# Block 4 of the output: six rows of 16 partitions stored in transfers of three partitions

## The chip, the cores and the metric

The kernel runs on one core of a Trainium2 chip. Its time is the device time of one execution in microseconds (us). Four runs of the kernel before took 162.29 to 163.43 us, with a median of 163.08. A further execution was taken by the hardware profiler: its time was 162.68 us and its span, from the first to the last instruction, 161.4 us.

## What is computed

A linear layer whose weight is built first, from a matrix, a low-rank product and a norm of each column:

```python
def reference(x, W, lora_A, lora_B, m, scale):
    W_adapted = W + scale * (lora_A @ lora_B)
    W_norm = np.sqrt(np.sum(W_adapted ** 2, axis=0, keepdims=True) + 1e-8)
    W_final = W_adapted / W_norm * m
    return (x.reshape(-1, 256) @ W_final).reshape(16, 2048, 256)
```

x has 32,768 rows of 256 float32 numbers, 33.55 MB, and the output is as large. W is 256 x 256, the rank is 16.

## The kernel before

**Blocks and chunks.** The rows are cut into 8 blocks of 4096. A block is 4 MB (4096 KB): 128 partitions with 32 rows each, and the 32 rows of a partition lie one behind the other in memory, 32 KB in one piece. A block has eight chunks of 4 rows per partition, so there are 64 chunks, g = 0 to 63. Five buffers in on-chip memory hold a block each (`x_bufs`); block b uses buffer b mod 5.

**The path of a chunk.** SP (SyncE) issues the loads of x. GpSimd rounds a pair of chunks to bf16 (L208). TensorE transposes it (L321), VectorE copies the transposed pair out of PSUM (L248), and TensorE multiplies it with the finished weight (L335). ScalarE (ACT) copies each product from PSUM back to where the chunk of x was (L276), so that the output of a block takes the place of its input in the buffer. At the last chunk of a store ACT drains (L282) and issues the store (L146). The loads stand in one queue (q1, from SP), the stores in another (q10, from ACT). Both are worked off by the same 16 DMA engines.

**The list of stores.** Each entry of `stores` has its first chunk, the number of chunks, the rows that one transfer takes, and the chunk after which ACT issues it. By number:

- 0 and 1: blocks 0 and 1, due at chunks 19 and 20
- 2 and 3: block 2 in two parts, due at chunk 24
- 4, 5 and 6: block 3, as four transfers of 4 rows, one of 4 rows, and one of 12 rows, due at chunks 27, 28 and 44
- 7: block 4, chunks 32 to 39, all 32 rows in one transfer of 4096 KB, due at chunk 44 together with store 6
- 8 and 9: blocks 5 and 6, due at chunks 47 and 55
- 10 and 11: block 7 in two halves, due at chunks 59 and 63

**Waits.** SP waits for stores 0 to 3 before it loads into their buffers again; GpSimd waits for store 2. Stores 4 to 11 have semaphores of their own (`late`), and nothing in the kernel waits for them but SP at the very end, at L360, one after the other. A transfer adds 16 to the semaphore of its store; `pieces` says what a store's semaphore has reached when all of it has landed.

**Where the change sits.** `transfer` cuts an entry into transfers of `rows` rows over all 128 partitions, and issues them on the engine that it is given.

Of the kernel before, what the change touches and what calls it, by code (L numbers as in the profile page):

```python
# [11 lines left out]
def kernel(  # L12
# [11 lines left out]
    P = 128  # L24
# [91 lines left out]
    stores = [(b * CH, CH, CH * J, 19 + b) for b in range(F - 1)]  # L116
    stores += [(G - CH, 3, 3 * J, G), (G - 5, 5, 5 * J, G)]
    FIRST = len(stores)
    stores += [(G, 4, J, G + 3), (G + 4, 1, J, G + 4)]
    stores += [(G + 5, CH - 5, (CH - 5) * J, 44), (G + CH, CH, CH * J, 44)]  # L120
    stores += [(b * CH, CH, CH * J, (b + 1) * CH - 1) for b in range(F + 2, NBLK - 1)]
# [1 line left out]

    def pieces(entry):

        return 16 * (entry[1] * J // entry[2])


    late = [nc.alloc_semaphore(f"store{n}") for n in range(FIRST, len(stores))]
    sems = {f"store{FIRST + k}": s for k, s in enumerate(late)}  # L130

    def sem(name):
        if name not in sems:
            sems[name] = tc.alloc_semaphore(name)
        return sems[name]

    def transfer(engine, name, entry, dram, store):
        g0, cnt, rows = entry[:3]
        b, c = divmod(g0, CH)
        (u0, ucnt), = [u for u in units if u[0] <= g0 < u[0] + u[1]]  # L140
        unit = dram[u0 * J * P : (u0 + ucnt) * J * P].rearrange("(p j) k -> p j k", p=P)
        for r in range(0, cnt * J, rows):
            here = x_bufs[b % XBUFS][:, c * J + r : c * J + r + rows, :]
            there = unit[:, (g0 - u0) * J + r : (g0 - u0) * J + r + rows, :]
            src, dst = (here, there) if store else (there, here)
            engine.dma_start(out=dst, in_=src).then_inc(sem(name), 16)  # L146

    def load_x(n):
        transfer(nc.sync, f"load{n}", loads[n], x_flat, False)

    def store_y(n):
        transfer(nc.scalar, f"store{n}", stores[n], out_flat, True)

    def wait_load(engine, g):
        engine.wait_ge(sem(f"load{load_of[g]}"), pieces(loads[load_of[g]]))

    def wait_store(engine, n):
        engine.wait_ge(sem(f"store{n}"), pieces(stores[n]))
# [3 lines left out]
        out=w_nat[:], in_=W.rearrange("(p t) o -> p t o", t=KC)  # L162
    ).then_inc(sem("load_w"), 16)
    nc.scalar.dma_start(
        out=a_nat[:], in_=lora_A.rearrange("(p t) r -> p t r", t=KC)
# [3 lines left out]
    for n in range(len(loads)):  # L169
# [14 lines left out]
        out=identity[:],  # L184
        in_=zeros[:],
# [7 lines left out]
    for p in range(1, NPR):  # L193
# [10 lines left out]
        if p == REST:  # L204
            wait_store(nc.gpsimd, FIRST - 2)
        if p >= NXB:
            nc.gpsimd.wait_ge(sem("turned"), p - NXB + 1)
        nc.gpsimd.tensor_copy(  # L208
            out=xb_bufs[p % NXB][:],
            in_=x_bufs[b % XBUFS][:, 2 * c * J : 2 * (c + 1) * J, :],  # L210
# [15 lines left out]
        out=wa[:], in0=ab_ps, scalar=float(scale), in1=w_nat[:], op0=ALU.mult, op1=ALU.add  # L226
# [19 lines left out]
    for p in range(NPR):  # L246
        nc.vector.wait_ge(sem("turned"), p + 1)
        nc.vector.tensor_copy(  # L248
            out=xt_bufs[p % NXT][:].rearrange("p r t -> p (r t)").bitcast(FP32),
            in_=xt_ps[p % 2][:],  # L250
# [4 lines left out]
    for engine, idle in ((nc.gpsimd, 8), (nc.vector, 24)):  # L255
# [13 lines left out]
        out=norm[:], in_=n2_ps, func=AF.Sqrt, bias=eps_col[:]  # L269
    ).then_inc(sem("act"), 1)  # L270
    drains = 0
    for g in range(NCH):
# [4 lines left out]
            out=x_bufs[b % XBUFS][:, c * J : (c + 1) * J, :], in_=y_ps[g % 2][:]  # L277
# [80 lines left out]
    for k, s in enumerate(late):  # L358
        nc.sync.wait_ge(s, pieces(stores[FIRST + k]))
        nc.sync.sem_clear(s)  # L360
# [35 lines left out]
```

## Time and profile before

| what | value |
|---|---|
| median of 4 runs (lowest, highest) | 163.08 us (162.29, 163.43) |
| profiled execution: time, span | 162.68 us, 161.4 us |
| PE (matmul) busy | 96.3 us, 60% of the span |
| ACT busy | 66.1 us, 41% |
| GpSimd busy | 60.8 us, 38% |
| VectorE busy | 45.0 us, 28% |
| HBM read, written | 33.85 MB, 33.55 MB |
| first, last issue of a load of x | 1.4 us, 85.8 us |
| first, last issue of a store | 47.0 us, 131.4 us |

Busy time is the sum of an engine's instructions without the issuing of DMAs. A row of digits on the page has one digit for each fortieth of the span, which here is 4.03 us; each is the busy share in tenths, and 9 is 90% or more. The DMA row is the mean over the core's 16 DMA engines. The compute engines have nothing more to do after 131.8 us; what follows is stores alone. Times inside the profile count from the start of the span.

### The profile page before, as it was taken

The numbers are of one execution on the slowest core, as the hardware profiler recorded it, in microseconds if no ns is written. First come the engines' busy times: TensorE is split into PE (matmuls) and PEld (weight loads), VectorE is DVE, ScalarE is ACT, GpSimd is POOL, SyncE is SP. The second block draws the span as 40 slices with busy tenths as digits, with TensorE's granted clock in tenths as the row PEclk, the third lists the DMA queues.
The fourth block names the chain that finished last, engine by engine and source line by source line (L and its number), as shares of the span: only waits on it lengthen the run. The fifth ranks groups of instructions, "written<-read, shape, count | busy, mean of one in ns | idle before, by whom it ended". The sixth has DMA issues, their size and how long they took to land. (4 is left out here: it accounts for less than half of the span.)

```text
span 161.4 us, 2027 instructions
## 1 busy us (share of the span) xinstructions
PE 96.3 (60%) x786; PEld 85.0 (53%) x786; DVE 45.0 (28%) x44; ACT 66.1 (41%) x68; POOL 60.8 (38%) x38
## 2 busy tenths in 40 slices
PE   0695936999999720000699999989997920000000
PEld 0284925899998610000689999979986910000000
DVE  0567322335353500000115354436353300000000
ACT  3411840686767450000056867766865740000000
POOL 1045319568685000001938685845829100000000
PEclk9999997899999995555559999999999997555555
DMA  4999999999999999989999999999999999999995
GB/s 158 427 455 463 390 504 406 390 495 414 422 390 455 422 422 439 439 370 447 412 418 425 436 418 425 447 419 424 440 484 398 439 457 400 439 455 406 410 430 223
DMA packets 4645, 67.43 MB, mean 418 GB/s; under 512 B 657, under 2 KB 674, under 8 KB 1698
## 3 DMA queue, kind: packets, MB, share of 16 engines
q1 hardware_dynamic: 2304, 33.82, 49.3%
q10 hardware_dynamic: 2338, 33.59, 48.9%
q14 instruction: 3, 0.02, 0.0%
HBM read 33.85 MB, written 33.55 MB: 418 GB/s over the span
## 5 line engine op out<-in xcount | busy, mean ns | idle before, releaser
L276 ACT COPY x_sb<-y_ps 128x1024 f32<-128x1024 f32 x64 | 62.3, 1014 | 58.8 <-PE y_ps L335 57.1
L208 POOL CAST xb<-x_sb 128x2048 bf16<-128x2048 f32 x31 | 58.4, 1893 | 63.9 <-DMA out_dram<-x_sb 24.7
L335 PE MATMUL y_ps<-w_final,xt 128*128 128x256 bf16 x512 | 64.6, 281 | 3.7 <-PEq L311 3.6
L248 DVE COPY xt<-xt_ps 128x1024 f32<-128x1024 f32 x32 | 39.1, 1225 | 75.2 <-PE xt_ps L321 75.0
L335 PEld LDWEIGHTS y_ps<-w_final,xt 128*128 128x128 bf16 x512 | 51.4, 101 | 11.4 <-issue 4.6
L321 PE MATMUL xt_ps<-identity,xb 128*128 128x128 f32 x264 | 37.3, 289 | 24.9 <-PEq L311 24.9
L321 PEld LDWEIGHTS xt_ps<-identity,xb 128*128 128x128 f32 x264 | 32.7, 151 | 26.4 <-issue 25.8
L292 PE MATMUL y_ps<-identity,a_nat 128*16 128x128 f32 x2 | 0.6, 396 | 4.1 <-DMA a_nat<-in_lora_A_dram 4.1
L264 ACT CAST xb<-x_sb 128x2048 bf16<-128x2048 f32 x1 | 1.9, 1898 | 2.5 <-DMA x_sb<-in_x_dram 2.5
L262 ACT ACT_TABLE_LOAD x1 | 1.3, 1283 | 2.4 <-issue 2.4
L292 PEld LDWEIGHTS y_ps<-identity,a_nat 128*16 128x16 f32 x2 | 0.1, 88 | 4.1 <-issue 4.1
L238 DVE RECIPROCAL rnorm<-norm 128x256 f32<-128x256 f32 x1 | 1.8, 1753 | 1.3 <-ACT norm L268 1.3
L305 PE MATMUL y_ps<-sq,ones 128*128 128x256 f32 x4 | 2.1, 674 | 0.0
L214 POOL MEMSET xb<- 128x2048 bf16 x1 | 1.8, 1804 | 0.0
L305 PEld LDWEIGHTS y_ps<-sq,ones 128*128 128x128 f32 x4 | 1.2, 324 | 0.8 <-DVE sq L229 0.7
L301 PE MATMUL y_ps<-m_row,ones 1*128 1x256 f32 x2 | 1.2, 709 | 0.5 <-DMA m_row<-in_m_dram 0.5
L220 DVE CAST b_bf<-b_nat 16x256 bf16<-16x256 f32 x1 | 0.3, 281 | 3.5 <-DMA b_nat<-in_lora_B_dram 3.5
L268 ACT ACTIVATE norm<-y_ps,eps_col 128x256 f32<-128x256 f32 x1 | 0.5, 474 | 1.6 <-PE y_ps L305 1.6
L296 PE MATMUL y_ps<-b_bf,aT 16*128 16x256 bf16 x2 | 0.6, 404 | 0.8 <-DVE aT L222 0.8
L301 PEld LDWEIGHTS y_ps<-m_row,ones 1*128 1x128 f32 x2 | 0.5, 305 | 1.0 <-DMA m_row<-in_m_dram 1.0
L225 DVE SCALAR_TENSOR_TENSOR wa<-y_ps,w_nat 128x512 f32<-128x512 f32 x1 | 0.7, 691 | 0.8 <-PE y_ps L296 0.8
L296 PEld LDWEIGHTS y_ps<-b_bf,aT 16*128 16x128 bf16 x2 | 0.1, 107 | 1.2 <-DVE aT L222 1.2
(14 smaller groups left out, 4.4 us busy)
## 6 DMA issues: line engine op xcount, KB each, us to landing
out_dram<-x_sb ACTq DMA_DIRECT2D x5, 4096.0 KB, 26.8
x_sb<-in_x_dram SPq DMA_DIRECT2D x7, 2048.0 KB, 29.7
x_sb<-in_x_dram SPq DMA_DIRECT2D x3, 4096.0 KB, 29.9
out_dram<-x_sb ACTq DMA_DIRECT2D x2, 2048.0 KB, 30.1
x_sb<-in_x_dram SPq DMA_DIRECT2D x1, 3072.0 KB, 46.5
out_dram<-x_sb ACTq DMA_DIRECT2D x2, 1536.0 KB, 19.3
out_dram<-x_sb ACTq DMA_DIRECT2D x1, 2560.0 KB, 30.8
out_dram<-x_sb ACTq DMA_DIRECT2D x5, 512.0 KB, 38.1
```

Of the source, the lines that this page charges most:

```text
L208: nc.gpsimd.tensor_copy(out=xb_bufs[p % NXB][:], in_=x_bufs[b % XBUFS][:, 2 * c * J : 2 * (c + 1) * J, :],).then_inc(sem("rounded"), 1)
L214: nc.gpsimd.memset(xb_bufs[NPR % NXB][:], 0.0).then_inc(sem("rounded"), 1)
L225: nc.vector.scalar_tensor_tensor(out=wa[:], in0=ab_ps, scalar=float(scale), in1=w_nat[:], op0=ALU.mult, op1=ALU.add).then_inc(dv, 1)
L238: nc.vector.reciprocal(out=rnorm[:], in_=norm[:]).then_inc(dv, 1)
L248: nc.vector.tensor_copy(out=xt_bufs[p % NXT][:].rearrange("p r t -> p (r t)").bitcast(FP32), in_=xt_ps[p % 2][:],).then_inc(sem("copied"), 1)
L262: nc.scalar.activation(out=warm[:], in_=eps_col[:], func=AF.Sqrt)
L264: nc.scalar.copy(out=xb_bufs[0][:], in_=x_bufs[0][:, 0 : 2 * J, :]).then_inc(sem("early"), 1)
L276: nc.scalar.copy(out=x_bufs[b % XBUFS][:, c * J : (c + 1) * J, :], in_=y_ps[g % 2][:]).then_inc(sem("room"), 1)
L301: nc.tensor.matmul(mb_ps, ones[0:1, :], m_row[:], start=True, stop=True).then_inc(pe, 1)
L305: i = nc.tensor.matmul(n2_ps, ones[:], sq[:, t, :], start=(t == 0), stop=(t == KC - 1))
L321: i = nc.tensor.transpose(xt_ps[p % 2][:, j * P : (j + 1) * P], xb_bufs[p % NXB][:, j, :].bitcast(FP32), identity[:],)
L335: i = nc.tensor.matmul(y_ps[h][:, j, :], xt_bufs[p % NXT][:, r : r + P, t], w_final[:, t, :], start=(t == 0 and (j % (J // 2)) == 0), stop ...
```

## The change

The transfer of store 7 is cut in three parts. Its first 26 rows go out as before, over all 128 partitions. Of its last six rows, the 112 partitions from 16 on are one transfer. The first 16 partitions are five transfers of three partitions and one of a single partition, with 18 KB and 6 KB. So eight transfers take the place of one, and `pieces` counts 16 x 8 for this store. All of them are issued by ACT, in this order, at the same place as before. No other load or store is changed, and no other instruction.

```diff
     stores += [(G - CH, 3, 3 * J, G), (G - 5, 5, 5 * J, G)]
     FIRST = len(stores)
+
+    UNEVEN, ODD = FIRST + 3, 6
     stores += [(G, 4, J, G + 3), (G + 4, 1, J, G + 4)]
...
     def pieces(entry):
 
+        if entry is stores[UNEVEN]:
+            return 16 * 8
         return 16 * (entry[1] * J // entry[2])
...
             src, dst = (here, there) if store else (there, here)
-            engine.dma_start(out=dst, in_=src).then_inc(sem(name), 16)
+            parts = [(0, P, 0, rows)]
+            if (g0, cnt, rows) == stores[UNEVEN][:3]:
+
+
+                q = rows - ODD
+                parts = [(0, P, 0, q), (16, P - 16, q, ODD)]
+                parts += [(p0, 3, q, ODD) for p0 in range(0, 15, 3)] + [(15, 1, q, ODD)]
+            for p0, n, r0, k in parts:
+                engine.dma_start(
+                    out=dst[p0 : p0 + n, r0 : r0 + k, :],
+                    in_=src[p0 : p0 + n, r0 : r0 + k, :],
+                ).then_inc(sem(name), 16)
```

## The prediction, made before the changed kernel ran

> **What bounds the kernel now.** I read the DMA rows first, since the page has no compute engine above 60% busy, then the queues, then the last microseconds in narrow windows.
>
> From the page of the kernel before (the fourth line gives packets and bytes; the last two give each queue's share of 16 engines' span):
>
> ```profile
> span 161.4 us, 2027 instructions
> ...
> DMA  4999999999999999989999999999999999999995
> GB/s 158 427 455 463 390 504 406 390 495 414 422 390 455 422 422 439 439 370 447 412 418 425 436 418 425 447 419 424 440 484 398 439 457 400 439 455 406 410 430 223
> DMA packets 4645, 67.43 MB, mean 418 GB/s; under 512 B 657, under 2 KB 674, under 8 KB 1698
> ## 3 DMA queue, kind: packets, MB, share of 16 engines
> q1 hardware_dynamic: 2304, 33.82, 49.3%
> q10 hardware_dynamic: 2338, 33.59, 48.9%
> ```
>
> The reader is to see a 9 in every slice between the first and the last. The loads (q1) and stores (q10) together fill 98.2% of 16 engines' span, 158.5 us of 161.4. Each engine carries a sixteenth of the bytes, 4.21 MB, so it runs at 26.6 bytes per ns and rests only at the start and the end. Nothing in the middle can be saved except bytes, and the change keeps all bytes. What is left is how evenly the 16 engines finish. Windows at the end show it (columns: window, its length, busy time of PE, PEld, DVE, ACT and POOL, clock, DMA share, GB/s; a packet is counted in the window where it starts):
>
> ```profile
> 158.50:159.10 0.60, 0.00 (x0) 0.00 (x0) 0.00 (x0) 0.00 (x0) 0.00 (x0) 0.50 1.02 437
> 159.10:159.40 0.30, 0.00 (x0) 0.00 (x0) 0.00 (x0) 0.00 (x0) 0.00 (x0) 0.50 0.39 164
> 159.40:159.80 0.40, 0.00 (x0) 0.00 (x0) 0.00 (x0) 0.00 (x0) 0.00 (x0) 0.50 0.30 123
> 159.80:160.20 0.40, 0.00 (x0) 0.00 (x0) 0.00 (x0) 0.00 (x0) 0.00 (x0) 0.50 0.00 0
> 160.20:160.60 0.40, 0.00 (x0) 0.00 (x0) 0.00 (x0) 0.00 (x0) 0.00 (x0) 0.50 0.10 41
> ```
>
> 164 GB/s for 0.30 us is three packets of 16 KB, 123 for 0.40 us is three more, 41 for 0.40 us is one. So nine engines have begun their last packet by 159.10, and one begins it alone after 160.20. The records of single packets are finer. On one engine a packet starts 4 ns before the one ahead of it ends, so that they string into 16 chains. These end, from the span's start, at 159.32 to 159.62 (ten of them), 159.79, 159.90, 159.98, 160.27, 160.31 and 160.86 us. Half a microsecond later the last write is confirmed and the span ends. The last chain sets the time; the mean of all lies about 1.2 us ahead of it. Three chains are late because each carried one 8 KB instruction fetch of 309 ns (the 159.98, 160.27 and 160.31 ones); the last has no fetch but a train of packets 40 to 127 ns too long.
>
> **The change, by engine.** Only store 7 differs: block 4, 32 rows, issued at 105.35 us, whose data moves from about 121 to 132 us. By then the loads are almost done (the last of them lands at 120.1) and q10 alone feeds the engines.
>
> The packet records give a cost by size: 4096 B 159 ns, 8192 B 309, 16384 B 611, 32768 B 1213. That is 8.4 ns plus 36.8 ns per 1000 bytes. A semaphore write takes 9 ns. Hence 26 rows (26,624 B) take 987 ns and six rows (6,144 B) 234 ns.
> - Before, each engine: 8 x 1213 + 9 = 9713 ns.
> - After, an engine outside the first three: 8 x 987 + 9, and of the 112 partitions seven packets, 7 x 234 + 9. Sum 9552 ns, **0.16 us less**. (Six rows of one partition less is 0.23; the more numerous packets take 0.07 back.)
> - After, engine 0: that, and 6 x (234 + 9) = 1458 ns, so **1.30 us more** than before. Engines 1 and 2 take five of the small transfers: 1215 ns, so **1.05 us more**.
>
> The three-partition transfers are not in this trace. The nearest row is the load of m: one partition, one data packet of 1024 B, and two updates of its semaphore, 4.05 us apart, where a load over 128 partitions shows sixteen. So few partitions mean few engines here. The Trainium skill ("DMA: Bandwidth & Descriptors", on why a DMA increments its semaphore by 16) says the number of engines is the largest divisor up to 16 of the slowest dimension, and that they are the lowest-numbered: three for 3, sixteen for 112, one for 1. I go by that.
>
> **Where a rule speaks against the change.** The row: stores 4, four transfers of 512 KB, are 32 KB per engine each, and between them a chain has 9 ns of semaphore write and then the next packet. A 4096 B packet is 159 ns there, on its line. The rule, in the same page's "Rules for kernel authors": coalesce, under 64 KB one pays mostly overhead. "SBUF — State Buffer", in "The DMA setup-cost knee", puts it at about 2 us fixed for every transfer. The six small transfers have 6 or 18 KB. By the rule they would cost engines 0 to 2 some 6 x 2 = 12 us, and the end would be at about 172; by the row it is 6 x 0.243 = 1.5. The row holds a queue that is never empty, as here, and that fixed cost is latency of completion, which no one waits for: of store 7 only SP's closing wait (L360) asks. I take 1.5.
>
> A second rule: the same SBUF page ("Door 1: The DMA port swizzle") ties partitions to 16 ports. If the 112 partitions go out as seven consecutive ones per engine, several engines meet at one port. Worked out from that port table, with equal sharing, the seven packets take about 2.1 us on average and 2.5 to 2.9 at worst, instead of 1.64: an estimate of +0.5 to +1.3 us. The nearest row is the load of lora_B: 16 partitions, all on four ports by that table. Five of its 1024 B packets start within 32 ns, beside x loads, and 15 of its 16 take 46 or 47 ns, the plain cost of that size. I take nothing and keep 1.3 as the upper end.
>
> **What is hidden.** ACT issues seven more transfers at about 106 us. Issues on this line take 0.34 us, or about 1.25 (four of ACT's 15 do), so 2.4 to 8.8 us of ACT. Behind them stand the copies of chunks 45 to 47, store 8, and through the freed PSUM buffers TensorE, whose later results ACT and the stores need. The cover is the queue. Store 8 is issued at 109.2 and its data starts at 130.1, store 9 at 119.7 for 139.8, store 11 at 131.4 for 154.3. That is 20 us of lead in each case, so this costs nothing up to 20. SP's waits on stores 0 to 3 and POOL's on store 2 are over before, and all loads are issued by 85.8. Nothing was waiting and nothing is freed sooner.
>
> **Sum.** If the last chain is none of engines 0 to 2, it ends at 160.86 - 0.16 = 160.70. Engine 0 is the one with m's packet. I can follow that chain except for a tie among three, which end at 159.54, 159.61 and 159.62. It goes to 160.84 to 160.92. Engines 1 and 2 I cannot name. From the early ten they would go to 160.37 to 160.67, from the 160.3 pair to 161.3. So the end moves from 160.86 to about 160.9: **+0.05 us**. The profiled run took 162.68, of which 161.4 is span; the median of the four runs, 163.08, lies 0.4 above it. I add the difference to the median: **163.1 us**.
>
> **The rivals.** Under 0.5% (0.8 us) a measurement of this kernel can hardly be told from no change.
> - *Forecast: engine 0 takes over as last, at the same time* (chance 0.58). The relief is worth at most 0.16, the burden 1.30 against a lead of 1.25 to 1.32. Its own range is 162.8 to 163.7, the upper end for an engine 1 or 2 out of the 160.3 pair.
> - *Slower: the last chain is itself engine 1 or 2* (0.22). Then 160.86 + 1.05, or 164.1. It decides once engine 1 or 2 ends within 0.23 us of the last chain; the next late ones, at 160.3, miss that. For it: two of the fifteen unnamed chains are these, and whatever holds the last one up may belong to its place. Against it: that is 2 in 15 by count alone.
> - *Slower: ports* (0.10). 163.6 to 164.4 by the second rule, over the bound from 0.8 us of stretch on the last engine. Against it, lora_B's packets.
> - *Faster: the first three are all ahead by 1.5 us in most executions* (0.07). Then everything else ends 0.16 earlier, 162.9; over 0.5% it would need late chains that come by chance and don't come again. The 162.29 run shows that ends vary by 0.8.
> - *The change doesn't do what it says* (0.03): the small transfers are spread over all engines. Each then has its old bytes and a few more packets, 163.2.
>
> Slower by over 0.5%: 0.22, most of the ports' 0.10, and a few in a hundred of the forecast, 0.35. Faster by over 0.5%: 0.04. The rest, 0.61, within. The range is 162.6 to 164.4: the forecast with its spread at the low end, both slower cases at the high end.
>
> **What would show it.** 112 + 16 more packets of 6144 B at 234 ns; DMA share still 1.0 from 121 to 158 us; stores 8 to 11 landing with the first engine 0.16 earlier and the last no later than before. In the end windows three packets should start late, near 160.2, not one. Packets of 6144 B well over 234 ns mean ports; a single last chain near 161.9 means engine 1 or 2 was the late one. Idle DMA between 121 and 158 us would mean that ACT's issues were not covered, and this sum would be wrong.

## The result, and the profile after

The changed kernel has a median of 163.2 us (162.55 to 165.62, 42 runs), beside 162.92 us for the kernel before (162.29 to 163.66, 63 runs). The ratio is 1.0034, with a 95% interval of 1.0020 to 1.0047: slower by about 0.55 us, inside the 0.5% that was called no change, though the interval lies above 1. Executions more than 1.5% above a kernel's fastest are left out of each ratio, here the one of 165.62. The forecast was 163.1 us.

The list of times says more than the ratio. 31 of the 42 executions lie between 162.55 and 163.88, with a median of 163.13, which is 0.21 above the kernel before. The other 11 lie between 164.10 and 165.62, with a median of 164.44, 1.5 above it. The kernel before has none as late: here and in all series below it never took more than 163.9 us. (31 x 0.21 + 11 x 1.5) / 42 is 0.55. So there are two differences, a small one of the main group and a large one in a quarter of the executions, the late group.

The profiled execution took 162.99 us, so it belongs to the larger group. Its page, with the rows that answer to those shown of before:

```profile
span 161.7 us, 2034 instructions
...
DMA  4999999999998999999999999999999898999995
...
DMA packets 4805, 67.43 MB, mean 417 GB/s; under 512 B 689, under 2 KB 706, under 8 KB 1858
...
q1 hardware_dynamic: 2304, 33.82, 49.5%
q10 hardware_dynamic: 2498, 33.59, 48.7%
```

The bytes are the same. There are 160 packets more, 128 of them between 2 and 8 KB (1858 - 706 beside 1698 - 674): the 112 + 16 packets of 6144 B. The DMA engines are full as before. In the packet records nearly all of these 128 packets take 234 ns, and none over 258.

The windows at the end of the same execution (columns as in the prediction):

```profile
158.50:159.10 0.60, 0.00 (x0) 0.00 (x0) 0.00 (x0) 0.00 (x0) 0.00 (x0) 0.50 1.02 437
159.10:159.40 0.30, 0.00 (x0) 0.00 (x0) 0.00 (x0) 0.00 (x0) 0.00 (x0) 0.50 1.15 492
159.40:159.80 0.40, 0.00 (x0) 0.00 (x0) 0.00 (x0) 0.00 (x0) 0.00 (x0) 0.50 0.20 82
159.80:160.20 0.40, 0.00 (x0) 0.00 (x0) 0.00 (x0) 0.00 (x0) 0.00 (x0) 0.50 0.39 164
160.20:160.60 0.40, 0.00 (x0) 0.00 (x0) 0.00 (x0) 0.00 (x0) 0.00 (x0) 0.50 0.29 123
160.60:160.90 0.30, 0.00 (x0) 0.00 (x0) 0.00 (x0) 0.00 (x0) 0.00 (x0) 0.50 0.13 55
```

123 GB/s for 0.40 us and 55 for 0.30 us are three packets of 16 KB and one: four engines start their last packet after 160.20, where before it was one. The small transfers now name three of the chains, since engine 0 has 13 packets of 6144 B, engines 1 and 2 have 12, and all others 7. Engine 0 ends at 161.17 us, engines 1 and 2 at 161.07 and 161.24, and the fourth chain, at 160.98, is the chain with the long train of slow packets. Everyone else is done by 160.53.

That the last chain ends 0.38 us later than the 160.86 of the trace before is not all due to the change. On average over the 16 engines, the data of store 7 starts at 120.86 us in the trace before and at 121.16 here, so 0.30 was lost ahead of the first changed transfer. The records put the loss at about 47 to 51 us, where both kernels issue the same transfers and store 7 is still far off. A second trace of the changed kernel, below, has lost 0.24 in the same place, a third only 0.07. Whether the small difference of 0.21 between the lists comes from the change is therefore open.

ACT's issues, from the timeline (start, length, engine, line, operation; in brackets how long the engine had been idle), first of the trace before, then of the trace after:

```profile
104.98 0.82 ACTq L146 DMA_DIRECT2D out_dram<-x_sb  x2
...
105.85 1.93 ACT L276 COPY x_sb<-y_ps 128x1024 f32<-128x1024 f32 x2 [0.98 <-ACTq L282]
...
107.00 1.03 PE L335 MATMUL y_ps<-w_final,xt 128*128 128x256 bf16 x8 [0.56 <-PEq L311]
...
109.20 0.34 ACTq L146 DMA_DIRECT2D out_dram<-x_sb  x1
```

```profile
104.67 3.26 ACTq L158 DMA_DIRECT2D out_dram<-x_sb  x9
...
107.97 1.93 ACT L291 COPY x_sb<-y_ps 128x1024 f32<-128x1024 f32 x2 [3.41 <-issue]
...
109.12 1.03 PE L350 MATMUL y_ps<-w_final,xt 128*128 128x256 bf16 x8 [3.00 <-PEq L326]
...
111.31 0.37 ACTq L158 DMA_DIRECT2D out_dram<-x_sb  x1
```

Nine issues take 3.26 us where two took 0.82. ACT's gap between copies, the issuing included, grows from 0.98 to 3.41 us, and TensorE's from 0.56 to 3.00. Store 8 is issued at 111.31 instead of 109.20. All of it is hidden: the data of store 8 starts at 130.4, and the DMA share is 1.02 and 1.03 in the windows of 128.6 to 130.6 and 130.6 to 132.6 us. The queue covers it as forecast.

### The profile page after: what moved, and what is told of

Read it like the earlier page. It is cut to its first block, busy times and chain, and to the rows that moved or that the text cites. A ratio compares the mean times of both kernels' runs of the same rounds, so it can differ in the third digit from the quotient of the medians.

```text
span 161.7 us, 2034 instructions
## 1 busy us (share of the span) xinstructions
PE 95.1 (59%) x786; PEld 84.0 (52%) x786; DVE 44.9 (28%) x44; ACT 66.1 (41%) x68; POOL 60.9 (38%) x38
## 2 busy tenths in 40 slices
DMA packets 4805, 67.43 MB, mean 417 GB/s; under 512 B 689, under 2 KB 706, under 8 KB 1858
## 5 line engine op out<-in xcount | busy, mean ns | idle before, releaser
L336 PE MATMUL xt_ps<-identity,xb 128*128 128x128 f32 x264 | 36.0, 282 | 24.3 <-PEq L326 24.3
L336 PEld LDWEIGHTS xt_ps<-identity,xb 128*128 128x128 f32 x264 | 31.7, 147 | 25.5 <-issue 25.0
L256 DVE TENSOR_TENSOR w_final<-wam,rnorm 128x256 bf16<-128x256 f32 x2 | 0.8, 422 | 0.0
```

The source lines that it names most:

```text
L336: i = nc.tensor.transpose(xt_ps[p % 2][:, j * P : (j + 1) * P], xb_bufs[p % NXB][:, j, :].bitcast(FP32), identity[:],)
```

## The experiments

Theory *load*: only the bytes and packets per engine count, so the time follows from the chain that ends last. Its rivals were *transfer* (the small transfers cost as such), and, from the first results on, *range* (transfers that do not span all 128 partitions let engines meet and slow each other) and *burst* (many semaphore writes in close order hold an engine up). Unless said otherwise, an edit is one of the changed kernel; where it alters the number of transfers, `pieces` is set to match. A chain is the string of packets of one DMA engine; "too long" means beyond the plain cost of a packet's size.

**The same eight transfers, with even load.**

```diff
-                parts += [(p0, 3, q, ODD) for p0 in range(0, 15, 3)] + [(15, 1, q, ODD)]
+                parts += [(0, 16, q + r0, 1) for r0 in range(ODD)]
```

> Eight transfers for block 4, as in the change, but the six rows of the first 16 partitions go out as six transfers of one row over all 16 partitions, so that every DMA engine has one packet of each and the same bytes as before. Theory 'load' (only the bytes per engine count): each engine gets 8 x 987 + 7 x 234 + 6 x 46 ns and eight semaphore writes of 9 ns instead of 9713 ns, 0.17 us more, so +0.1 to +0.25 us (ratio 1.001), and no execution more than 1 us above the median. Rival 'transfer' (the number of small transfers costs, in issue or completion): the same +0.3% as the change or more, and the same group of executions at about 164.3 us.

Measured: ratio 1.0053 (1.0028 to 1.0078), five of 13 executions at 164.2 to 165.6. Load alone fails: without any unevenness the kernel is at least as slow as the change. In the trace, itself a late execution of 164.22 us, one chain's packets of the 112-partition transfer are up to 472 ns too long, 1.5 us in sum.

**Twice the rows, and half.**

```diff
-    UNEVEN, ODD = FIRST + 3, 6
+    UNEVEN, ODD = FIRST + 3, 12
```

> The change with twelve rows in place of six: the same eight transfers, twice the bytes in the small ones. Theory 'load': engine 0 has 2.43 us more than in the kernel before, engines 1 and 2 1.96 us more, the others 0.39 us less. Engine 0 then ends at about 162.0 us of the span, engines 1 and 2 at 161.3 to 162.3: +1.1 to +1.5 us (ratio 1.007 to 1.009), with a group of executions near +2.2. In the profile exactly three chains of packets end last, over 1 us behind all others. Rival 'transfer': no more than the change, +0.3%.

Measured: 1.0147 (1.0105 to 1.0189), about 1 us over what load gives. Three chains do end last, at 163.60, 162.28 and 162.23 us. Engines 1 and 2 are where they should be. Engine 0 is 1.3 us beyond it: its last three small packets are 291, 281 and 718 ns too long, and in the same three microseconds another chain, outside the first three, has packets 295, 701 and 307 ns too long. Here, then, small packets are stretched, and the other chain's are already those of the next store.

> The change with three rows in place of six. Theory 'load': engine 0 has 0.73 us more than before, engines 1 and 2 0.61 us more, the others 0.05 us less. From ends of 159.6 (engine 0) and 159.4 to 160.3 (engines 1 and 2) they come to 160.3 and 160.0 to 160.9, where the last chain of the kernel before ends: ratio 1.000 to 1.002, and a smaller and closer group of slow executions, at about +0.7 us. Rival 'transfer': +0.3% as the change, since the number of transfers is the same.

(The number is 3 here.) Measured: 1.0004 (0.9987 to 1.0021), and none of 14 executions over 163.72. The trace has engines 0 to 2 at 160.23 to 160.31, the train chain last at 160.71. This is load's sum, and it excludes a fixed price of these eight transfers that could make up the change's 0.55 us. It also has a 112-partition transfer, of three rows, and no late execution, so the cut as such is not enough: how long it lasts counts.

**Marks for the engines.**

```diff
+                parts = [(0, P, 0, q, 0, OUT), (0, P, q, ODD, 64, OUT)]
+                p0 = 0
+                for n in list(range(1, 16)) + [8]:
+                    parts.append((p0, n, q, ODD, 0, 64))
+                    p0 += n
```

(ODD is 1, and the two last numbers are columns.)

> The kernel before, but for the last row of block 4: columns 64 to 255 go out as one transfer over 128 partitions, columns 0 to 63 as 16 small ones over 1, 2, 3, up to 15 and then 8 partitions. If a transfer of n partitions runs on the n lowest engines, an engine's number can be read from its count of 256 B packets: 16 for engine 0, 15 for engine 1, down to none for engine 15. If lateness belongs to a place, the instruction fetches sit on engines 1 and 2, as in the trace of the change, and one other, and the engine with the long train of slow packets is above 2. If it comes by chance, they sit elsewhere here. Time: +0.1 to +0.4 us over the kernel before, from 0.43 us more on engine 0.

Measured: one run at 164.87 us, 1.85 over the runs before, far more than expected. The counts of 256 B packets come out as 16, 15, 13 and so on down to 0, except that three chains were not told apart. Most chains with nine marks or more have their next two packets of 32768 B too long, by 0.9 to 1.7 us in sum; those with few marks mostly do not. That is burst's picture, at about 0.1 us a mark, from one trace and with a doubt over those chains. It takes more than the six small transfers of the change: in the trace after, engine 0 loses 0.19 us behind them, engines 1 and 2 nothing. The first instruction fetch, at 86.7 us, is on the chain with 15 marks, engine 1, as far as that chain can be followed. The train's chain has 12 by count, and it is one of those in doubt.

**The cut alone, and 112 + 16 with even load.**

```diff
-                parts = [(0, P, 0, q), (16, P - 16, q, ODD)]
-                parts += [(p0, 3, q, ODD) for p0 in range(0, 15, 3)] + [(15, 1, q, ODD)]
+                parts = [(0, P, 0, q), (0, P, q, ODD)]
```

> Block 4 in two transfers, 26 rows and 6 rows, both over all 128 partitions: the cut alone. Every engine has 8 x 987 + 8 x 234 + 2 x 9 ns instead of 9713, 0.07 us more. Theory 'load' and both of its additions below: ratio 1.000 to 1.001, no execution more than 0.8 us above the median.

Measured: 1.0012 (0.9997 to 1.0028), none of 22 executions over 163.86.

```diff
-                parts += [(p0, 3, q, ODD) for p0 in range(0, 15, 3)] + [(15, 1, q, ODD)]
+                parts += [(0, 16, q, ODD)]
```

> Block 4 in three transfers: 26 rows over 128 partitions, six rows over the partitions 16 to 127, six rows over the partitions 0 to 15, one on each engine. Even load and few semaphore writes: 0.08 us more on every engine. Theory 'range' (where a transfer does not span all 128 partitions, engines meet at partitions that are another's in the 128-partition transfers, and in some executions slow each other down): ratio 1.002 to 1.005, a fifth or more of the executions over 1 us above the fast ones. Theory 'burst' (more than five or six semaphore writes in close order hold an engine up): ratio 1.000 to 1.001 and no such group, as with load alone.

Measured: 1.0031 (1.0011 to 1.0052), six of 22 executions at 164.0 to 166.4. Four of these six are left out of the ratio, so it understates the effect. Between these two kernels only the grouping of the same six rows differs, and with it comes the late group, as often as in the change. Range passes; load and burst do not. The trace of this kernel is of an execution of 162.67 us, so its late ones were not seen packet by packet.

**The changed kernel twice more.**

> The changed kernel once more, for a second trace. Three in four: about 163.1 us, with engines 0 to 2 (the chains with 13, 12 and 12 packets of 6144 B) ending last within 0.3 us of each other. One in four: about 164.3, and then the chain that ends last shows what that group is: 'load' has the long train of slow packets on engine 0, 1 or 2; 'range' has two chains with packets stretched by 0.1 to 0.7 us each between 129 and 135 us of the span, 1 us or more in sum.

> The changed kernel a third time; the same expectations as for the second trace. In both, if instruction fetches keep their places, engines 1 and 2 carry one each.

Measured: 162.99 us and 164.71 us. The first repeats the trace after: engines 0 to 2 end at 160.90, 160.92 and 161.18, the train chain at 161.16. The second is one of the late group. Its end windows:

```profile
160.20:160.60 0.40, 0.00 (x0) 0.00 (x0) 0.00 (x0) 0.00 (x0) 0.00 (x0) 0.50 0.00 0
160.60:161.00 0.40, 0.00 (x0) 0.00 (x0) 0.00 (x0) 0.00 (x0) 0.00 (x0) 0.50 0.29 123
161.00:161.40 0.40, 0.00 (x0) 0.00 (x0) 0.00 (x0) 0.00 (x0) 0.00 (x0) 0.50 0.29 123
161.40:162.40 1.00, 0.00 (x0) 0.00 (x0) 0.00 (x0) 0.00 (x0) 0.00 (x0) 0.50 0.08 33
```

In each window of 0.40 us, 123 GB/s are three packets of 16 KB, and 33 for 1.00 us are two: after 160.60, when all others have begun their last packet, three chains still have eight packets to go. What put them there stands in the packet records of 128.5 to 133 us. Each line is one chain, with its end in us and its packets in bytes; +n is how many ns a packet took over its size's plain cost:

```
163.05  26624, sem, 6144+372, 6144, 6144+58, 6144+224, 6144+238, 6144, 6144+419, sem, small+95, 4 small
162.53  26624+356, sem, 6144+30, 6144+231, 6144+71, 6144+213, 6144+276, 6144+414, 6144, sem
162.01  6144 x6, 6144+578, sem, 6 small
160.47  6144, 6144+296, 6144+401, 6144 x4, sem
160.76  6144 x7, sem, 5 small
159.23  6144 x7, sem
```

Apart from one small packet, 95 ns too long, and one of 26,624 B, the stretched packets are those of the 112-partition transfer. The first two chains are stretched in the same three microseconds, by 1.4 and 1.6 us, one of them engine 1 or 2 and the other outside the first three. The train is on the chain that ends at 160.63, outside the first three again. The third is engine 0, 0.6 us too long. So this late execution is range's, not load's. That all 11 are of this kind is not shown: this is the only late trace of the changed kernel.

**The uneven load without the 112.**

```diff
+                parts = [(0, P, 0, q), (0, P, q, ODD)]
+                extra = [(p0, 3) for p0 in range(0, 15, 3)] + [(15, 1)]
...
+            for p0, n in extra:
+                engine.dma_start(
+                    out=scratch[p0 : p0 + n], in_=src[p0 : p0 + n, q : q + ODD, :]
+                ).then_inc(sem(name), 16)
```

> The uneven load without the 112-partition transfer: block 4 in 26 and 6 rows over all 128 partitions, and besides, the six rows of the first 16 partitions are stored a second time, into a scratch buffer, by the change's six small transfers (96 KB more are written). Engine 0 has 1.53 us more than in the kernel before, engines 1 and 2 1.29, the others 0.07. If the change's slow executions come from the 112-partition transfer alone: engines 0 to 2 end at about 161.0 to 161.5 us, +0.2 to +0.6 us (ratio 1.001 to 1.004), no execution over 164.3, and no 6144 B packet over 350 ns. If they come from the small transfers: a group of executions over 1 us above the median, as with the change.

Measured: 1.0010 (0.9991 to 1.0029), none of 13 executions over 163.88, no 6144 B packet over 259 ns. Engines 0 to 2 end at 161.38 to 161.49, where load's sum puts them, and the train's chain at 161.64. Although it moves more bytes than the change, burdens the three engines as much and has ACT issue as many transfers, it has no late group.

**A larger dose of the ranges.**

```diff
+                parts = [(16, P - 16, 0, rows), (0, 16, 0, rows)]
```

> All 32 rows of block 4 in two transfers, over the partitions 16 to 127 and 0 to 15: even load, 0.01 us more per engine by count, and no small transfers. Theory 'range': the time in which engines can meet is 7 x 1.2 us long in place of 7 x 0.23, so that most executions lose 1 us or more, ratio 1.006 to 1.02, with packets of 32768 B in the window 121 to 134 us stretched by 0.3 us or more on two or more chains. 'Load' and 'burst': ratio 1.000.

Measured: 1.0308 (1.0282 to 1.0334). The direction is range's and the size is beyond it. 112-partition packets are stretched here and there, by 0.05 to 1.5 us. The single 32 KB packet of each engine in the 16-partition transfer is stretched on most engines, by 0.6 to 4.7 us.

```diff
+                parts = [(0, P, 0, q), (0, 64, q, ODD), (64, 64, q, ODD)]
```

> Block 4 in 26 rows over 128 partitions, and six rows over the partitions 0 to 63 and 64 to 127, two transfers with four packets per engine each: even load, 0.08 us more per engine by count. If engines slow each other by sharing partitions' ports, as the port table of 64-partition transfers has it, two engines meet at each port all the time: 6144 B packets at about 450 ns in place of 234, +1.5 to +2 us, ratio 1.009 to 1.012. If what matters is that 112 is cut unlike the others, 234 ns and ratio 1.000 to 1.001.

Measured: 1.0039 (1.0019 to 1.0058), between the two expectations, with two of 14 executions at 164.3 and 164.7. Most 6144 B packets take 234 ns, but ten of 128 take over 300, up to 947. If the port table holds for these transfers, two engines at one port are not slow at once; meetings that stretch single packets exist here as well.

**Sixteen partitions, eight apart.** All else is the kernel before:

```diff
+            if (g0, cnt, rows) == (G + CH, CH, CH * J):
+                for k in range(8):
+                    engine.dma_start(
+                        out=dst[k : P : 8], in_=src[k : P : 8]
+                    ).then_inc(sem(name), 16)
+                continue
```

> Block 4 in eight transfers of 16 partitions each, all 32 rows, the partitions of one transfer eight apart (k, k + 8, up to k + 120): each engine has the same eight packets of 32768 B as in the kernel before and seven more semaphore writes, 0.06 us more. In the run with 112 and 16 partitions the packets of the 16 neighbouring partitions took 1.0 to 4.7 us too long on most engines. If nearness of the partitions did that (16 engines inside 512 KB of the output and inside one eighth of the buffer's partitions), these packets take 1213 ns as before and the ratio is 1.000 to 1.001. If the port table of the 128-partition transfers decides, sixteen partitions eight apart lie on eight ports, two engines meet at each, and the packets take about 2400 ns: +5 to +10 us, ratio 1.03 to 1.06. In between: any transfer cut otherwise than over 128 partitions loses where engines meet by chance, 1.003 to 1.02.

Measured: 1.0499 (1.0458 to 1.0540), 8 us more. Two windows of this kernel, then the same two of the kernel before:

```profile
121.00:131.00 10.00, 10.00 (x94) 9.33 (x93) 4.42 (x5) 7.59 (x8) 6.52 (x4) 1.00 1.02 255
131.00:141.00 10.00, 3.82 (x35) 3.26 (x33) 0.72 (x1) 3.85 (x4) 0.00 (x0) 0.91 0.96 279
```

```profile
121.00:131.00 10.00, 8.19 (x74) 7.27 (x72) 2.45 (x2) 6.67 (x8) 4.63 (x3) 1.00 0.99 427
131.00:141.00 10.00, 0.00 (x0) 0.00 (x0) 0.00 (x0) 0.33 (x1) 0.00 (x0) 0.71 0.99 424
```

The share of busy engines is about 1 in both, but the bytes fall from 427 to 255 GB/s: the engines count as busy while their packets take longer. How, the packets of one chain show, k = 0 to 7 from left to right:

```
32768  32768+674  32768+1329  32768+1566  32768  32768+162  32768+1328  32768+1554
```

The plain cost is 1213 ns, so here the third and fourth packets of each group of four take about twice their time, and the first nothing extra. The second varies between the chains, from nothing extra to 1.3 us. The pattern starts anew at k = 4 in about ten of the 16 chains; in the others the fifth packet is 0.6 to 1.2 us too long as well. In the port table of the Trainium skill ("SBUF — State Buffer", section "Door 1: The DMA port swizzle") four neighbouring partitions share a port: the transfers k = 0 to 3 use eight of the 16 ports, and k = 4 to 7 the other eight. The period of four, where it shows, agrees with it, and so does the rate of the later packets in each four, two engines to a port. It looks as if an engine gets about one packet of 32 KB into a crowded stretch before it is held up. That would explain why short stretches, as most of those of the 64-partition cut, cost nothing; no run here tests it.

No version was measurably faster than the kernel before.

## Why the prediction was right, and which step of it failed

The time, 163.1 against 163.2 us, and the forecast of no change were right; the account of where the difference comes from was half right. Part of the agreement in the time is luck. The forecast was 0.05 us more than a median of 163.08 from four runs; the measured medians are 0.28 apart, from 162.92, and the ratio gives 0.55.

- *The cost per packet* held to the nanosecond (234 ns for 6144 B), and the sums per engine with it. In the uneven kernel without the 112 the three engines end in that run's expected range of 161.0 to 161.5.
- *Which engines take the small transfers* held: one chain has six of the small packets and two have five. The rule that the prediction takes from the Trainium skill ("DMA: Bandwidth & Descriptors", "Why a DMA increments its semaphore by 16 and not by 1") is, exactly, about the slowest dimension that is not of size 1. So "one for 1" does not follow from it for one partition with six rows; that this transfer went to one engine, as one packet of 6144 B, is what the trace shows.
- *Engine 0 takes over as last* held in part. In two of the three traces of the change it and engines 1 and 2 end within 0.3 us of each other, but the last is engine 1 or 2, 0.07 and 0.28 us after engine 0. The forecast put engines 1 and 2 early unless they came "out of the 160.3 pair". In these traces, as far as the chains can be followed, each of the two carries an instruction fetch, as did the chains that ended at 159.98, 160.27 and 160.31 before. So the change burdens two engines that have less lead than the average. Less the 0.30 and 0.24 us lost before store 7, the last chain would end at 160.94 in both traces: an estimate, and close to the forecast of 160.9, though on another engine.
- *ACT's issues are hidden*: 2.44 us more of issuing, inside 2.4 to 8.8, and covered.
- *The rule of about 2 us per small transfer* was rightly set aside: half the rows with the same eight transfers cost nothing. But the row that it was weighed against has four transfers, and 16 in close order did cost something, 1.85 us in one run.
- *The late chain is engine 1 or 2* (0.22) didn't occur. In each trace in which small packets mark the first three engines, the train is on an unmarked chain; the run with marks on all leaves its place open. In the late trace engine 1 or 2 does end last, but by its stretched packets, without the train.
- *Ports* (0.10) is the step that failed. The prediction says "I take nothing and keep 1.3 as the upper end". The term was set at nothing in the sum. The runs show it paid in about a quarter of the executions, 11 of 42, neither always nor never; there it is 1.4 and 1.6 us on the two stretched chains and 1.5 us in the time, somewhat above the estimate of 0.5 to 1.3. That it is the ports which are shared is not shown. lora_B's packets were no fair test: they are one packet of 1 KB for each engine, and in the last experiment the first packet of 32 KB takes its plain time on most engines.
- The range holds the median, which lies inside the forecast's own 162.8 to 163.7 as well. It does not hold the late group: six of its 11 executions are above 164.4.
- One figure is off without consequence: the mean of the 16 chain ends before is 159.74, 1.1 us ahead of the last, not 1.2.

What stays open: which partitions of the 112 each engine takes, and so why one execution has the meetings and the next has none. Chains that enter the 112 late are the ones stretched in the late execution, but equally late ones pass clean in others. That the shared resource is the port is supported by the period of four, in about ten of 16 chains; a limit at the output's addresses, which repeat with the same period, isn't excluded.

## What to carry to other kernels

When the DMA engines are full and every transfer spans 128 partitions, cutting out a range of partitions to shift 0.16 us of load can make engines hold each other up, and that cost about ten times the gain in a quarter of the executions here. The same rows cut over all 128 partitions showed no such group. Compare the whole list of times, not its middle: here the medians differ by 0.28 us and a quarter of the executions by 1.5. And a row that is to bound a collision should be as long as the case: three rows on 112 partitions showed no late execution in 14, six rows 11 in 42, and 32 rows only late ones, four of four.

## What the hardware did that was not expected

- In three traces of the change and in the doubled one, two of the three 8 KB instruction fetches are on engines 1 and 2, at about 87 us and at 137 to 140 us, and the third, at 131 to 137 us, on an engine outside the first three, as far as the chains can be followed. The places seem to be fixed.
- One engine has a train of packets 40 to 130 ns too long between about 119 and 136 us in nearly every trace, about 0.5 to 0.8 us in sum. It is what the kernel before ends on. Its cause wasn't looked for.
- Full DMA share is no proof of full rate: 16 partitions eight apart kept it at 1.02 with 255 GB/s.
